# First layer of a hybrid decoder step: one tile shape for neighbouring small products, block-diagonal inverses, sample state update in 32-row tiles

## The chip, the cores and the metric

The kernel runs on one core of one Trainium2 chip. The metric is the device time of one execution in microseconds (us), as a median of runs. Engines are named as in the profile: PE is TensorE's matmul, PEld its weight load, DVE is VectorE, ACT is ScalarE, POOL is GpSimd, SP the queue of SyncE that starts DMAs.

## The reference, cut to what matters

One inference step over two layers, for a prompt of 256 tokens and a sample of 8 batches with 8 tokens each (320 rows together). Only layer 0's mixer matters here: a gated delta net (4 heads of 128) and RWKV-7 (8 heads of 64) side by side. Both are linear recurrences worked out in chunks of 64 tokens: four chunks for the prompt, and one for the sample, in which the eight batches are eight blocks of 8 rows.

```python
# gated delta net, one chunk; RWKV-7 has the same structure with other decays
lmat = jnp.where(strict, bb[..., :, None] * kkt * decay, 0.0)
rhs = bb[..., None] * (vb - gam[..., None] * jnp.einsum('bhck,bhkv->bhcv', kb, s))
u = lax.linalg.triangular_solve(lmat + eye, rhs, left_side=True, lower=True, unit_diagonal=True)
o = gam[..., None] * jnp.einsum('bhck,bhkv->bhcv', qb, s) + jnp.einsum('bhij,bhjv->bhiv', qkt, u)
s_new = jnp.exp(glast)[..., None] * s + jnp.einsum('bhck,bhcv->bhkv', kb * jnp.exp(glast - gcum)[..., None], u)
```

So each chunk needs the inverse of a unit lower triangular 64x64 matrix, products of that inverse with right-hand sides, and a step of the state from chunk to chunk. The sample's states (8 batches) take one step each.

## The kernel before

All weights stream through SBUF in columns of 128. `dense` multiplies them in two float32r parts (hi, lo) with two-part activations: 24 products of 128x128 weights with 256 or 320 columns for each column block. They write the PSUM tiles `pd` and `pe`.

The mixer of layer 0 (`even_in`) lays the small float32 products of the recurrences between those dense ones. After each three dense products `between[0]` runs `step`, which takes the next piece of one of three lanes: `g_lane` (gated delta net, `gdn_unit`, PSUM tag `pG`, tiles `g_...`), `r_lane` (RWKV, `rwkv_solve` and `rwkv_scan`, PSUM tag `pR`, tiles `r_...`) and `set_lane` (`rwkv_setup`). Four units go through each lane. A piece's turn comes by `pe[0]`, an estimate of PE's time that `mm` adds up. PE runs its instructions in this order. A float32 product stands in the trace as two records.

A product's tile shape is written K*M below: K rows of the contraction (partitions of both operands), M columns of the stationary operand (partitions of the output). PE is used in the shapes 128\*128, 128\*64, 64\*128, 64\*64 and 32\*128. The shape follows from the operands' partitions:

- Two chunks share 128 partitions. Chunk c has the rows of half c % 2 (`chunk_rows`), so a product of one chunk alone contracts over 64 rows: K is 64. In `gdn_unit` these are `g_vk` with the inverse, and all products with `g_uw`, the corrected values and keys.
- `solve` inverts by doubling: blocks of 2, 4, ... 64. At each level l it makes two products for each pair of chunks and head, against `n1` and against `t`. For the prompt `u` and `x` hold two chunks in columns of their own between zeros, so K is 128 and M 64. The sample's chunk has tiles of its own (`invs`, `xs`) on 64 partitions, so its products at levels 1 and 2 are 64\*64.
- In `rwkv_scan` a state `z` has one head in each half of the partitions, so its products (`r_zs` with `r_step`, `r_ar` with `r_zs`) are 64\*64, one for each half.
- The sample's state update of the delta net multiplies `kd` (64 rows) with `um`, the corrected values masked to four batches, 64\*128 with 512 columns, twice a unit.

Each unit's results go to `og` and `orw`. When all lanes are done, the output projection starts (`out_proj`, dense again), and with it the fetch of the memory attention's keys and values (`mkv`), which the SP queue issues in program order.

Of the kernel before, what the change touches and what calls it, by code (L numbers as in the profile page):

```python
# [26 lines left out]
def _constants():  # L27
    """Masks and selections that depend on shapes alone: name -> [128, n]."""
# [27 lines left out]
    c["bm8"] = (j[:, None] // 8 == np.arange(8)[None, :]) * 1.0  # L56
    c["sel8"] = (p[:, None] % 32 == np.arange(8)[None, :]) * 1.0
# [12 lines left out]
    even = ("blk64", "triP", "triS", "blkS", "maskP", "maskS", "negP", "negS", "id64", "lev", "lev0T", "bm8", "sel8", "scan")  # L70
# [36 lines left out]
def _lay(inp):  # L107
    """Rearranges the inputs for the device: no arithmetic."""
# [61 lines left out]
def _unlay(r):  # L170
    """Device outputs -> the reference's shapes."""
# [27 lines left out]
def trunk(ctx: ExitStack, tc: tile.TileContext, A, O, phases=None):  # L199
# [86 lines left out]
    def load_log_exp():  # L286
        """The table of Ln and Exp, behind all that was laid out before."""
# [6 lines left out]
    def sigmoid(out):  # L294
        """From out = exp(-x), by functions that share a table."""
# [21 lines left out]
    # ---------------------------------------------------------------- the stream of weights  # L317
# [40 lines left out]
    def weights(kt):  # L358
        """The two parts of the plan's next columns."""
# [6 lines left out]
    def dense(a, kt=KT):  # L366
        """The next 128 columns w of the plan: psum [128, n] = w^T a over kt K-tiles."""
# [5 lines left out]
        if first:  # L373
            # the tensor engine's clock rises with use: zeros keep it at work until the operands are there
# [18 lines left out]
    def split(dst, src, scale=1.0):  # L393
        """dst (hi, lo) = the two parts of src * scale."""
# [37 lines left out]
    class Prep:  # L432
        """Splits x * gain tile by tile for the next products; 1/rms comes later, on their results."""
# [13 lines left out]
    def dense_norm(prep, n, use, kt=KT):  # L447
        """n dense tiles of prep.a; 1/rms is worked out behind the first two of them."""
# [11 lines left out]
    def out_proj(o, nxt):  # L460
        """x += w^T o; the next block's operand is prepared tile by tile."""
# [13 lines left out]
    def weave(main, filler, every=1):  # L475
        """main with a step of the filler after each few of its own, then the filler's rest."""
# [14 lines left out]
    # ---------------------------------------------------------------- feed-forward  # L491
# [88 lines left out]
    # ---------------------------------------------------------------- memory tokens and attention  # L580
# [5 lines left out]
    def mem_kv(layers):  # L586
        """k (feature-major) and v (token-major) of the prompt's memory, into their outputs."""
# [57 lines left out]
    class Mem:  # L645
        """A memory block; its tiles are opened, and the caches' keys fetched, ahead of its turn."""
# [29 lines left out]
    def mem(m, prep, nxt):  # L676
# [17 lines left out]
        def softmax_rows(ps, p):  # L694
            """p = softmax(ps / 16) over the last axis; ps, p [128, nh, 256]."""
# [12 lines left out]
        def s_score(g):  # L708
            # rows (head, batch of four, query): a zero-padded query block for each batch
# [137 lines left out]
    def shaped(a, shape):  # L847
        """a [p, n] seen as [p, *shape]."""
# [3 lines left out]
    def tiles_of(pool, prefix):  # L852
        """t(name, *shape): a tile of a pool in which names share a slot of pad columns by a tag."""
# [13 lines left out]
    def solve(n1, u, x, us, xs, t, bank):  # L867
        """Blocks of 64: the transpose u of (1 - N)^-1 from n1 = N^T + 1 [128, 3, nh, 64], N strictly lower.
        Two chunks share a block of 128 partitions: u and x [128, 2, nh, 2, 64] hold them in columns of their
        own, between zeros, so that one product serves both. The sample's chunk [64, nh, 64] stands alone.  # L870
        At level l the inverses x of blocks of 2^l are joined by pairs; u = x^T changes in the second
        columns of each pair alone, and x, of blocks up to 32, is u with each block of 32 transposed."""
# [3 lines left out]
        def half(a, l, i):  # L876
            """Of the columns of a [..., 64], those with bit l = i."""
# [4 lines left out]
        def pack(a, l):  # L882
            """Their places side by side."""
# [4 lines left out]
        def wide(m, r, n):  # L888
            """A mask or the like [128, ...] for n blocks of rows r."""
# [3 lines left out]
        def views():  # L893
            """Places of 32 columns: the heads' chunks, each head in rows of its own; the sample's."""
            ps = bank()
            return (ps[:, :128].rearrange("p (b o n) -> p b o n", b=2, o=2),
                    ps[:64, 128:128 + 32 * nh].rearrange("p (h n) -> p h n", h=nh))

        low, all_ = H2[0], slice(0, 128)
# [10 lines left out]
        for l in range(1, 6):  # L910
            tt = t()
# [4 lines left out]
            pt, pts = views()  # L916
            for b in two:
                for h in range(nh):
                    mm(pack(pt[H2[h], b].rearrange("p o n -> p (o n)"), l), n1[:, b, h], half(x[:, b, h], l, 0))
            for h in range(nh):  # L920
                for o in two:
                    V.tensor_mul(half(tt[H2[o], :2, h], l, 0), pack(pt[H2[h], :, o], l), wide(lev, H2[h], 2))
            if l < 3:
# [1088 lines left out]
```

## Time and profile before

| | before |
|---|---|
| median of 3 runs | 1482.69 us (1482.44 to 1484.91) |
| profiled execution: span from first to last instruction | 1481.2 us |
| PE busy / PEld busy | 1420.0 us (96%) / 1240.4 us (84%) |
| DVE / ACT / POOL busy | 915.3 / 671.0 / 280.8 us |
| mean granted TensorE clock | 0.954 |

The profiled execution is the only one with a trace, and its span is its time; the runs' median is 1.5 us above it. A busy PE is not PE at its peak: matmuls are pipelined, and a record's duration overlaps the next record's. How fast PE goes through products is read from the starts of neighbouring records. The granted clock is 1.0 at 2.4 GHz and 0.5 at 1.2 GHz; a value between them is a mean over a stretch that has both.

### The profile page before, as it was taken

Reading aid. Unit: us, or ns where it says so; the run is one execution under the profiler, and the core shown is the slowest. Engines: PE = TensorE matmul, PEld = TensorE weight load, DVE = VectorE, ACT = ScalarE, POOL = GpSimd, SP = SyncE. Lnnn points to the kernel's source line nnn. Section 1 sums busy time; section 2 is a strip of 40 time slices with the busy share of each in tenths; the row PEclk is TensorE's granted clock in tenths of the full one; section 3 lists DMA queues with packets and bytes.
Section 4 is the critical chain, followed back from the end, with each engine's and each line's share of the span. In section 5 each row is a group of like instructions: output and inputs, shape, how many; then the busy total and the mean of one; then the engine's idle time right before and its main releaser. Section 6 shows DMA issues by size and latency. Waiting matters only on the chain. (4 is left out here: it accounts for less than half of the span.)

```text
span 1481.2 us, 29014 instructions
## 1 busy us (share of the span) xinstructions
PE 1420.0 (96%) x11071; PEld 1240.4 (84%) x11071; DVE 915.3 (62%) x1916; ACT 671.0 (45%) x1497; POOL 280.8 (19%) x542
## 2 busy tenths in 40 slices
PE   8999999999999899999999999999789999999997
PEld 7798787786896796999999997766359879999997
DVE  6986864764854553566656646684765545666564
ACT  6745434254443442544434535563354335444343
POOL 5532531432411200111100110003011001110001
PEclk9999988889988899999999999999789999999999
DMA  5333232133522856444576747998959644444443
GB/s 215 121 106 119 85 96 80 46 106 94 194 86 64 310 202 264 133 152 152 179 228 204 236 142 269 337 344 298 405 186 383 212 196 145 155 142 157 146 146 100
DMA packets 81485, 268.04 MB, mean 181 GB/s; under 512 B 9346, under 2 KB 21890, under 8 KB 76866
## 3 DMA queue, kind: packets, MB, share of 16 engines
q1 hardware_dynamic: 64450, 247.21, 48.9%
q10 hardware_dynamic: 16896, 18.98, 3.9%
q8 instruction: 87, 1.43, 0.4%
q14 instruction: 52, 0.43, 0.1%
HBM read 254.26 MB, written 11.90 MB: 180 GB/s over the span
## 5 line engine op out<-in xcount | busy, mean ns | idle before, releaser
L284 ACT ACTIVATE whi<-raw 128x512 fp32r<-128x512 f32 (+1 forms) x541 | 308.0, 616 | 382.7 <-PE pd L270 160.8
L344 DVE TENSOR_TENSOR wlo<-raw,whi 128x512 fp32r<-128x512 f32 (+1 forms) x541 | 383.0, 745 | 81.0 <-ACT whi L284 78.4
L270 PE MATMUL pd<-ahi,whi 128*128 128x320 f32 (+2 forms) x1336 | 420.2, 316 | 9.1 <-ACT ahi L284 5.0
L270 PE MATMUL pd<-ahi,wlo 128*128 128x320 f32 (+1 forms) x1328 | 416.4, 314 | 3.7 <-DVE wlo L344 3.6
L270 PE MATMUL pd<-alo,whi 128*128 128x320 f32 (+2 forms) x1336 | 416.8, 315 | 2.1 <-DVE alo L301 2.1
L270 PEld LDWEIGHTS pd<-ahi,whi 128*128 128x128 f32 (+1 forms) x1336 | 257.7, 193 | 22.2 <-ACT ahi L284 6.8
L270 PEld LDWEIGHTS pd<-ahi,wlo 128*128 128x128 f32 x1328 | 256.9, 193 | 14.0 <-issue 6.1
L270 PEld LDWEIGHTS pd<-alo,whi 128*128 128x128 f32 (+1 forms) x1336 | 256.3, 193 | 14.2 <-issue 7.1
L270 PE MATMUL pe<-alo,whi 128*128 128x320 f32 x416 | 129.7, 312 | 0.0
L270 PE MATMUL pe<-ahi,wlo 128*128 128x320 f32 x416 | 129.1, 310 | 0.5 <-DVE wlo L344 0.5
L270 PE MATMUL pe<-ahi,whi 128*128 128x320 f32 x416 | 128.7, 310 | 0.0
L519 POOL TENSOR_TENSOR fw<-fw 128x320 f32<-128x320 f32 x44 | 39.0, 886 | 332.9 <-DVE fw L518 303.6
L420 POOL TENSOR_TENSOR acc<-acc,w 128x320 f32<-128x320 f32 (+1 forms) x48 | 47.2, 982 | 240.2 <-ACT w L284 237.9
L270 PEld LDWEIGHTS pe<-ahi,wlo 128*128 128x128 f32 x416 | 78.1, 188 | 1.5 <-DVE wlo L344 1.4
L270 PEld LDWEIGHTS pe<-alo,whi 128*128 128x128 f32 x416 | 78.1, 188 | 0.5
L270 PEld LDWEIGHTS pe<-ahi,whi 128*128 128x128 f32 x416 | 78.0, 188 | 0.3
L270 PE MATMUL pe<-fhi,whi 128*128 128x320 f32 x176 | 54.3, 309 | 0.0
L270 PE MATMUL pd<-fhi,whi 128*128 128x320 f32 x176 | 54.3, 309 | 0.0
L270 PE MATMUL pe<-fhi,wlo 128*128 128x320 f32 x176 | 54.3, 309 | 0.0
L270 PE MATMUL pe<-flo,whi 128*128 128x320 f32 x176 | 54.3, 309 | 0.0
L270 PE MATMUL pd<-fhi,wlo 128*128 128x320 f32 x176 | 54.3, 309 | 0.0
L270 PE MATMUL pd<-flo,whi 128*128 128x320 f32 x176 | 54.3, 309 | 0.0
(460 smaller groups left out, 2283.4 us busy)
## 6 DMA issues: line engine op xcount, KB each, us to landing
pg<-in_kv SPq DMA_DIRECT2D x107, 512.0 KB, 6.6
raw<-in_w_fi SPq DMA_DIRECT2D x88, 512.0 KB, 3.6
mkv<-in_mkv SPq DMA_DIRECT2D x32, 1024.0 KB, 9.3
raw<-in_w_fo SPq DMA_DIRECT2D x32, 512.0 KB, 3.6
raw<-in_w_sb SPq DMA_DIRECT2D x24, 512.0 KB, 3.7
raw<-in_w_gp SPq DMA_DIRECT2D x16, 512.0 KB, 3.5
raw<-in_w_mk SPq DMA_DIRECT2D x16, 512.0 KB, 3.6
raw<-in_w_mv SPq DMA_DIRECT2D x16, 512.0 KB, 3.6
```

The costliest lines, as they stand in the source:

```text
L270: nc.tensor.matmul(out, lhsT=lhsT, rhs=rhs, start=start, stop=stop, skip_group_check=True)
L284: S.activation(out, in_, f, **kw)
L344: V.tensor_sub(lo[:, ks], raw[:, ks], hi[:, ks])
L420: P.tensor_add(self.acc, self.acc, self.sq)
L519: P.tensor_mul(u, u, st["g"])
```

## The change

Products that stand beside each other get the same tile shape, by operands that are padded with zeros to all 128 partitions:

- `solve` takes the sample's chunk as a third block of the same tiles `u` and `x`, with zeros in the upper 64 rows of `n1`, `u` and `t`. Its products are 128\*64, and its masks, copies and first transposes are done with those of the prompt.
- In `gdn_unit` the inverses of both chunks of a pair, side by side, are one stationary of 128\*128 (`both`). `uw` is one tile for all units with a place for each half and zeros beside it, so all products of the scan are 128\*128. `rows` and `sel` are padded from 8 to 128 rows.
- In `rwkv_scan` the corrections use the pair's inverse as 128\*128, and `z` becomes two column blocks, each head's state with zeros in the other head's rows: products of 128\*64. Its final write is two DMAs instead of one.
- The sample's state update masks `uv` once, by the batch's place in its half (`bm4`), and multiplies 32 rows with 32 rows: two products of 32\*128.

Comments and docstrings are dropped too, which the diff below leaves out.

```diff
-    def solve(n1, u, x, us, xs, t, bank):
+    def solve(n1, u, x, t, bank):
...
-        for o in two:
-            P.memset(u[H2[o], :, :, 1 - o], 0.0)
+        P.memset(u[H2[0], :, :, 1], 0.0)
+        P.memset(u[H2[1], :, :, 0], 0.0)
+        P.memset(u[H2[1], 2, :, 1], 0.0)
         for h in range(nh):
             for o in two:
-                r = H2[o]
-                V.tensor_mul(u[r, :, h, o], n1[r, :2, h], wide(cc("lev0T"), r, 2))
-            V.transpose(x[:, :, h], u[:, :, h])
-        V.tensor_mul(us, n1[low, 2], wide(cc("lev0T"), low, nh))
-        V.transpose(xs, us)
+                nb = 3 - o
+                V.tensor_mul(u[H2[o], :nb, h, o], n1[H2[o], :nb, h], wide(cc("lev0T"), H2[o], nb))
+        V.transpose(x, u)
...
+            if nb == 3:
+                P.memset(tt[H2[1], 2], 0.0)
...
-            for b in two:
+            pt = bank()
+            for b in range(nb):
                 for h in range(nh):
-                    mm(pack(pt[H2[h], b].rearrange("p o n -> p (o n)"), l), n1[:, b, h], half(x[:, b, h], l, 0))
+                    y = x[:, b, h] if b < 2 else x[:, b, h, 0]
+                    mm(pack(place(pt, h, b), l), n1[:, b, h], half(y, l, 0))
...
-                for h in range(nh):
-                    mm(pack(pts[:, h], l), n1[low, 2, h], half(xs[:, h], l, 0))
-                V.tensor_mul(half(tt[low, 2], l, 0), pack(pts, l), wide(lev, low, nh))
...
+            if l < 2:
+                V.transpose(x, u)
...
+            uw = st_even["uw"] = ep.tile([128, 2, 2, 2, 128], F32, name="g_uw")
+            for o in range(2):
+                P.memset(uw[H2[1 - o], :, o], 0.0)
...
-        for c in range(4):
-            r, b, cs = chunk_rows(c)
-            mm(pu[r, b].rearrange("p a n -> p (a n)"), inv[r, b, 0, c % 2], vk[r, b].rearrange("p a n -> p (a n)"))
-        act(uw, pu)
+        for b in range(2):
+            mm(pu[:, b].rearrange("p a n -> p (a n)"), both(b), vk[:, b].rearrange("p a n -> p (a n)"))
+        act(uw[H2[0], :, 0], pu[H2[0]])
+        V.tensor_copy(uw[H2[1], :, 1], pu[H2[1]])
...
-            mm(pz, kd[r, b], uw[r, b, 0], stop=c == 0)
+            mm(pz, kd[:, b], uw[:, b, o, 0], stop=c == 0)
...
-            um = t("um", 4, 128)[:64]
-            P.tensor_mul(um, bc(uv[:64, None, :], [64, 4, 128]), bc(cc("bm8")[:64, b4, None], [64, 4, 128]))
-            yield 1.2
+            b4, rows4 = slice(4 * q, 4 * q + 4), slice(32 * q, 32 * q + 32)
             pz = bank_g()
-            mm(pz, kd[:64, 2], um.rearrange("p b n -> p (b n)"))
+            mm(pz, kd[rows4, 2], um[rows4].rearrange("p b n -> p (b n)"))
...
+        pu = bank_r()[:, :512].rearrange("p (b h n) -> p b h n", b=2, h=2)
+        for b in range(2):
+            for h in range(2):
+                mm(pu[:, b, h], inv[:, b, h].rearrange("p o n -> p (o n)"), rhs[:, b, h].rearrange("p a n -> p (a n)"))
         for odd in range(2):
             rr = h2[odd]
-            pu = bank_r()[:, :512].rearrange("p (b h n) -> p b h n", b=2, h=2)
-            for b in range(2):
-                for h in range(2):
-                    mm(pu[rr, b, h], inv[rr, b, h, odd], rhs[rr, b, h].rearrange("p a n -> p (a n)"))
...
-                        mm(pz[h2[h]], step[h2[h], c - 1], z[h2[h]], start=False)
+                        mm(pz[h2[h]], step[:, c - 1], z[:, h], start=False)
...
-            z = t("zs", 64, bufs=2)
-            ts(z, pz, fac[:, c:c + 1], None, ALU.mult)
+            z = t("zs", 2, 64, bufs=2)
+            stt(z, bc(pz[:, None, :], [128, 2, 64]), fac[:, c:c + 1], cc("blk64").rearrange("p (h n) -> p h n", h=2),
+                ALU.mult, ALU.mult)
```

The order of instructions shows where PE's shape changes. First PE in the solve of unit 0, levels 1 and 2 of the inversion, of the kernel before. The sizes are those of the output; `r_xs`, `r_invs` and the 64x32 rows are the sample's, 64\*64, the `pd` rows are 128\*128, the others 128\*64.

```order
L270 MATMUL pd<-alo,whi 128x256
L270 MATMUL pR<-r_invs,r_t 64x32 x2
L270 MATMUL pR<-r_xinv,r_n_890 64x64
L270 MATMUL pG<-g_ux,g_t 64x32
L270 MATMUL pR<-r_xinv,r_n_890 64x64 x3
L270 MATMUL pG<-g_ux,g_n_1152 64x64 x2
L270 MATMUL pd<-ahi,whi 128x256
```

The same place of the changed kernel, where the sample's products follow those of the prompt, all 128\*64:

```order
L271 MATMUL pd<-alo,whi 128x256
L271 MATMUL pR<-r_inv,r_t 64x64
L271 MATMUL pd<-ahi,whi 128x256
L271 MATMUL pR<-r_inv,r_t 64x64 x3
L271 MATMUL pR<-r_inv,r_t 64x32 x2
L271 MATMUL pG<-g_ux,g_t 64x64 x2
L271 MATMUL pG<-g_ux,g_t 64x32
L271 MATMUL pd<-ahi,wlo 128x256
```

Five changes of shape became four, two of them around a single dense product that stands inside the group. The second place is the end of the mixer, unit 3, on PE of the kernel before: the corrections of RWKV (`r_rhs`, 64\*64) and of the delta net (`g_vk`, 64\*64).

```order
L270 MATMUL pR<-r_rhs,r_inv 64x128 x8
L270 MATMUL pR<-cst,r_sa 64x128
L270 MATMUL pR<-r_sav,r_g 64x64 x2
L270 MATMUL pG<-g_vk,g_ux 64x256 x4
L275 MATMUL pG<-cst,g_sa 64x128
```

And of the changed kernel:

```order
L271 MATMUL pR<-r_rhs,r_inv 128x128
L271 MATMUL pR<-cst,r_sa 64x128
L271 MATMUL pR<-r_sav,r_g 64x64 x2
L271 MATMUL pR<-r_rhs,r_inv 128x128 x3
L271 MATMUL pG<-g_vk,g_ux 128x256 x2
```

Twelve products became six of twice the output rows, and one of the four `r_rhs` products moved ahead of the sample's. The third place is the last six small products before the output projection, before:

```order
L270 MATMUL pR<-orw,cste 128x320
L270 MATMUL pR<-r_sm,r_bkt 64x512
L270 MATMUL pG<-g_um,g_kd 128x512
L270 MATMUL pR<-w,cste 128x320
L270 MATMUL pR<-r_s_151,r_lora 128x320
L270 MATMUL pG<-g_um,g_kd 128x512
L270 MATMUL pG<-w,cst 128x320
```

and now, where the two updates of the sample's states stand together:

```order
L271 MATMUL pR<-orw,cste 128x320
L271 MATMUL pR<-r_sm,r_bkt 64x512
L271 MATMUL pG<-g_um,g_kd 128x512 x2
L271 MATMUL pR<-w,cste 128x320
L271 MATMUL pR<-r_s_154,r_lora 128x320
L271 MATMUL pG<-w,cst 128x320
```

Counted over PE's whole instruction order of the mixer, up to its last small product: 473 changes of tile shape between neighbours before and 316 now, 988 small products before and 964 now. The `g_um` pair is adjacent in two units of the four. DVE has 44 instructions fewer in the whole kernel, ACT has 20 activations fewer and 4 DMAs more, POOL has 48 more, nearly all of them fills with zeros.

## Rows read from the trace of the kernel before

**Rows 1.** The page, the span in 40 equal slices of 37 us: PE's busy tenths, and the granted clock in tenths.

```profile
PE   8999999999999899999999999999789999999997
PEclk9999988889988899999999999999789999999999
```

**Rows 2.** Busy time by stretch. The columns are: from and to (us), length, busy us of PE, PEld, DVE, ACT and POOL with their instructions, granted clock, share of the DMA engines, GB/s.

```profile
8.00:490.00 482.00, 467.80 (x3390) 381.66 (x3388) 328.44 (x839) 228.69 (x604) 166.84 (x345) 0.90 0.33 106
...
60.00:82.00 22.00, 21.13 (x144) 17.70 (x143) 20.86 (x52) 12.20 (x27) 12.89 (x25) 1.00 0.41 135
82.00:92.00 10.00, 10.00 (x74) 9.70 (x75) 5.97 (x18) 1.22 (x4) 4.79 (x11) 0.68 0.19 61
181.00:209.00 28.00, 28.00 (x210) 25.46 (x209) 20.07 (x60) 11.36 (x28) 11.12 (x23) 0.76 0.26 85
243.00:273.00 30.00, 28.68 (x157) 18.36 (x156) 13.75 (x44) 9.45 (x27) 9.99 (x24) 0.55 0.08 22
403.00:420.00 17.00, 17.00 (x98) 14.92 (x98) 8.22 (x23) 2.29 (x5) 3.18 (x6) 0.60 0.14 46
468.00:490.00 22.00, 18.69 (x42) 8.01 (x42) 7.02 (x15) 4.91 (x9) 6.24 (x7) 0.50 0.11 42
490.00:495.00 5.00, 4.48 (x15) 4.08 (x16) 1.90 (x2) 0.20 (x1) 0.96 (x1) 0.50 0.88 287
```

**Rows 3.** Waits of PE from 8 to 490 us, the longest: who waited for whom, total us, times, longest.

```profile
PE pd L270 <- DVE r_e L1311: 2.6, 2, 1.8
```

**Rows 4.** PE in order of time at 2.4 GHz: start, us until the end, product, K*M, moving operand, records. Two groups of small products of one shape, the second between dense ones.

```profile
116.98 0.45 PE L270 MATMUL pR<-r_inv,r_t 128*64 128x64 f32 x8
117.26 0.40 PE L270 MATMUL pG<-g_ux,g_t 128*64 128x64 f32 x4
...
129.68 0.31 PE L270 MATMUL pd<-alo,whi 128*128 128x320 f32 x1
129.83 0.31 PE L270 MATMUL pd<-ahi,whi 128*128 128x320 f32 x1
130.06 0.45 PE L270 MATMUL pR<-r_xinv,r_n 128*64 128x64 f32 x8
130.35 0.40 PE L270 MATMUL pG<-g_ux,g_n 128*64 128x64 f32 x4
130.67 0.42 PE L270 MATMUL pd<-ahi,wlo 128*128 128x320 f32 x1
130.93 0.31 PE L270 MATMUL pd<-alo,whi 128*128 128x320 f32 x1
131.07 0.31 PE L270 MATMUL pd<-ahi,whi 128*128 128x320 f32 x1
```

**Rows 5.** The same view at three more places: the scan of unit 0, the last unit's corrections, and the sample's state update.

```profile
150.82 0.38 PE L270 MATMUL pG<-g_sc,g_step 128*128 128x128 f32 x2
151.14 0.43 PE L270 MATMUL pG<-g_g,g_uw 64*128 64x64 f32 x2
151.50 0.43 PE L270 MATMUL pG<-g_kq,g_sc 128*128 128x64 f32 x2
151.86 0.48 PE L270 MATMUL pG<-g_uw,g_kd 64*128 64x128 f32 x2
152.28 0.34 PE L270 MATMUL pR<-r_sav,xT 128*64 128x64 f32 x4
152.54 0.33 PE L270 MATMUL pR<-r_zs,r_step 64*64 64x64 f32 x4
152.81 0.34 PE L270 MATMUL pR<-xT,r_sav 128*64 128x64 f32 x4
...
456.32 1.36 PE L270 MATMUL pR<-r_rhs,r_inv 64*64 64x128 f32 x16
457.61 0.43 PE L270 MATMUL pR<-cst,r_sa 128*64 128x128 f32 x2
...
164.09 1.12 PE L270 MATMUL pG<-g_um,g_kd 64*128 64x512 f32 x2
165.14 0.41 PE L270 MATMUL pd<-alo,whi 128*128 128x320 f32 x1
```

**Rows 6.** The first products of the kernel, which multiply zeros (`zero`): PE in order of time, then two stretches with the columns of the second group (the number of PE records stands in brackets).

```profile
3.41 5.31 PE L270 MATMUL pd<-zero 128*128 128x320 f32 x12 [3.41 <-POOL r_e L1307]
...
3.50:7.00 3.50, 3.50 (x7) 2.32 (x8) 1.20 (x2) 1.64 (x4) 0.08 (x2) 1.00 0.93 339
7.00:8.30 1.30, 1.30 (x6) 0.88 (x6) 0.51 (x4) 1.30 (x4) 0.97 (x2) 1.00 1.04 415
```

**Rows 7.** PE in order of time where the clock has just fallen: a long run of narrow products, and two dense ones of 256 columns.

```profile
183.65 1.13 PE L270 MATMUL pR<-r_ar,r_z 64*64 64x16 f32 x16
...
189.42 0.41 PE L270 MATMUL pd<-ahi,whi 128*128 128x256 f32 x1
189.63 0.41 PE L270 MATMUL pd<-ahi,wlo 128*128 128x256 f32 x1
```

**Rows 8.** Groups of instructions from 8 to 490 us: a transpose at the start of `solve`, and a fill with zeros; behind the count the busy us and the mean ns of one, then the idle time ahead of them.

```profile
L906 DVE STREAM_TRANSPOSE r_xinv<-r_inv 128x256 f32<-128x256 f32 x8 | 3.0, 409 | 0.0
...
L901 POOL MEMSET r_inv<- 64x256 f32 x8 | 2.4, 305 | 14.7 <-PE pR L270 14.5
```

**Rows 9.** The end of the mixer: PE's first product of the output projection, and the first fetch for the memory attention on the SP queue.

```profile
490.25 0.64 PE L270 MATMUL pd<-ahi,whi 128*128 128x320 f32 x1 [3.56 <-ACT ahi L284]
...
491.93 0.33 SPq L662 DMA_DIRECT2D mkv<-in_mkv  x1
```

More of the change, by code (lines that the diff above doesn't have):

```diff
@@ L69, in _constants @@
     c["causal"] = np.where(p[None, :] < p[:, None], 0.0, NEG)
[L70 removed]
+    even = ("blk64", "triP", "triS", "blkS", "maskP", "maskS", "negP", "negS", "id64", "lev", "lev0T", "bm8", "bm4", "sel8", "scan")
     groups = []
@@ L920, in solve @@
+            pt = bank()
+            for b in range(nb):
+                for h in range(nh):
+                    y = x[:, b, h] if b < 2 else x[:, b, h, 0]
+                    mm(pack(place(pt, h, b), l), n1[:, b, h], half(y, l, 0))
             for h in range(nh):
                 for o in two:
-                    V.tensor_mul(half(tt[H2[o], :2, h], l, 0), pack(pt[H2[h], :, o], l), wide(lev, H2[h], 2))
-            if l < 3:
-                P.tensor_copy(half(tt[low, 2], l, 1), wide(one, low, nh))
-                for h in range(nh):
-                    mm(pack(pts[:, h], l), n1[low, 2, h], half(xs[:, h], l, 0))
-                V.tensor_mul(half(tt[low, 2], l, 0), pack(pts, l), wide(lev, low, nh))
@@ L928, in solve @@
-            yield HOP
-            pu, pus = views()
-            for b in two:
-                for h in range(nh):
-                    mm(pack(pu[H2[h], b].rearrange("p o n -> p (o n)"), l), tt[:, b, h], half(u[:, b, h], l, 1))
+                    n = nb if o == 0 else 2
+                    src = pt[H2[h], :64 * n].rearrange("p (b n) -> p b n", n=64)[:, :, 32 * o:32 * o + 32]
+                    V.tensor_mul(half(tt[H2[o], :n, h], l, 0), pack(src, l), wide(lev, H2[h], n))
+            yield HOP
@@ L933, in solve @@
+            pu = bank()
+            for b in range(nb):
+                for h in range(nh):
+                    y = u[:, b, h] if b < 2 else u[:, b, h, 0]
+                    mm(pack(place(pu, h, b), l), tt[:, b, h], half(y, l, 1))
             for h in range(nh):
                 for o in two:
-                    act(half(u[H2[o], :, h, o], l, 1), pack(pu[H2[h], :, o], l))
-                if l < 5:
-                    V.transpose(x[:, :, h], u[:, :, h])
-            if l < 3:
-                for h in range(nh):
-                    mm(pack(pus[:, h], l), tt[low, 2, h], half(us[:, h], l, 1))
-                act(half(us, l, 1), pack(pus, l))
-                if l < 2:
-                    V.transpose(xs, us)
+                    n = nb if o == 0 else 2
+                    src = pu[H2[h], :64 * n].rearrange("p (b n) -> p b n", n=64)[:, :, 32 * o:32 * o + 32]
+                    act(half(u[H2[o], :n, h, o], l, 1), pack(src, l))
+                if l < 5 and l > 1:
+                    V.transpose(x[:, :2, h], u[:, :2, h])
@@ L1096, in gdn_stats @@
             tr(pr[:8, 128 * b:128 * b + 128], rt[:, b])
-        rows = [ep.tile([8, NT], F32R, name=f"g_rows{i}") for i in range(2)]
-        split(rows, pr[:8, :NT])
+        rows = [ep.tile([128, NT], F32R, name=f"g_rows{i}") for i in range(2)]
+        for x in rows:
+            P.memset(x.bitcast(F32), 0.0)
+        split([x[:8] for x in rows], pr[:8, :NT])
         st_even.update(beta=beta, gcum=gcum, dec=dec, nbg=nbg, rows=rows)
@@ L1220, in gdn_unit, with both @@
         yield 0.8
-        ux = t("ux", 640, tag="kb")
-        inv, xinv = (shaped(ux[:, 256 * i:256 * i + 256], (2, 1, 2, 64)) for i in range(2))
-        invs, xs = (shaped(ux[:64, 512 + 64 * i:576 + 64 * i], (1, 64)) for i in range(2))
-        yield from solve(n1, inv, xinv, invs, xs, lambda: t("t", 3, 1, 64, bufs=2), bank_g)
+        ux = t("ux", 768, tag="kb")
+        inv, xinv = (shaped(ux[:, 384 * i:384 * i + 384], (3, 1, 2, 64)) for i in range(2))
+        yield from solve(n1, inv, xinv, lambda: t("t", 3, 1, 64, bufs=2), bank_g)
         oT = og[:, u]
-        uw = t("uw", 2, 2, 128)
-        pu = [bank_g().rearrange("p (b a n) -> p b a n", b=2, a=2) for _ in range(1)][0]
-        for c in range(4):
-            r, b, cs = chunk_rows(c)
-            mm(pu[r, b].rearrange("p a n -> p (a n)"), inv[r, b, 0, c % 2], vk[r, b].rearrange("p a n -> p (a n)"))
-        act(uw, pu)
+        def both(b):
+            return inv[:, b, 0].rearrange("p o n -> p (o n)")
+        uw = st_even["uw"]
+        pu = bank_g().rearrange("p (b a n) -> p b a n", b=2, a=2)
+        for b in range(2):
+            mm(pu[:, b].rearrange("p a n -> p (a n)"), both(b), vk[:, b].rearrange("p a n -> p (a n)"))
+        act(uw[H2[0], :, 0], pu[H2[0]])
+        V.tensor_copy(uw[H2[1], :, 1], pu[H2[1]])
         yield 0.3
@@ L1253, in gdn_unit @@
         pu = bank_g()
-        mm(pu[:64, :128], invs[:, 0], r1[:64])
+        mm(pu[:, :128], both(2), r1)
         uv = t("uv", 128)
-        act(uv[:64], pu[:64, :128])
+        act(uv, pu[:, :128])
         yield HOP
@@ L1556, in rwkv_scan @@
                 for h in range(2):
-                    mm(py[h2[h]], z[h2[h]], ar[h2[h], c, 1], start=False)
+                    mm(py[h2[h]], z[:, h], ar[:, c, 1], start=False)
             act(yT[:, cs], py)
-            z = t("zs", 64, bufs=2)
-            ts(z, pz, fac[:, c:c + 1], None, ALU.mult)
+            z = t("zs", 2, 64, bufs=2)
+            stt(z, bc(pz[:, None, :], [128, 2, 64]), fac[:, c:c + 1], cc("blk64").rearrange("p (h n) -> p h n", h=2),
+                ALU.mult, ALU.mult)
             yield HOP
-        S.dma_start(O["rwkv_p"][:, 64 * u:64 * u + 64], z)
+        for h in range(2):
+            S.dma_start(O["rwkv_p"][h2[h], 64 * u:64 * u + 64], z[h2[h], h])
         pz = bank_r()
```

66 lines of the change are left out of this document (38 added, 28 removed).

## Prediction

> **What bounds the kernel now.** I read the page's 40 slices first. PE is at 0.9 nearly everywhere, and the granted clock is below 0.9 in slices 6 to 9 and 12 to 14, and later in two more [rows 1]. The first thirteen slices are layer 0's mixer, the only part that the change touches. The stretch from 8 to 490 us says more: PE is busy for 467.80 of 482.00 us, so it idles for 14.2; DVE has 328.44, ACT 228.69, POOL 166.84; the clock is 0.90 [rows 2]. A clock of 0.90 means that (1 - 0.90) x 2 = 0.2 of the stretch, about 96 us, ran at 1.2 GHz. So PE is the bound, and its time holds two things beside plain work: the changes of shape between small products, and the slow clock. In two places another engine is near: from 60 to 82 us DVE is busy for 20.86 of 22.00 us [rows 2], and the longest waits of PE are for DVE's `r_e`, 2.6 us in two [rows 3]; and at the end of the mixer PE idles 3.56 us before the output projection [rows 9].
>
> What the mixer saves, the kernel saves: `mkv`'s fetch stands on SP behind the mixer, at 491.93 [rows 9], and the dense work after it follows in PE's order. So I look for one number, by how much 490 moves.
>
> **The price of a change of shape.** The rows of starts give it. Dense products follow each other at 0.15 us (129.68 to 129.83). From 129.83 there is an excursion to small products and back: dense, eight records of `r_xinv`, four of `g_ux`, dense, dense, up to 130.93: 1.10 us [rows 4]. Without the two changes it would take 2 x 0.147 for the two dense ones, 0.28 for eight records (116.98 to 117.26, where a group of the same shape follows), and the four. For those I have bounds: half of eight, 0.14, or by the pace of a 512-column record, 1.05 / 2 = 0.53 us (164.09 to 165.14 [rows 5]), so 0.066 for 64 columns and 0.26 for four. What is left is 0.27 to 0.39, or 0.135 to 0.195 a change. The scan gives the same by another way: at 150.82, 151.14, 151.50 and 151.86 runs of two records, each of another shape than the one before, take 0.32, 0.36, 0.36 and 0.42; at the 512-column pace (0.13 for two of 64 columns, 0.27 for two of 128) 0.05, 0.23, 0.23 and 0.15 are left, 0.165 on average [rows 5]. I take 0.15, in the middle of both.
>
> **Work that goes.** The order has 157 changes of shape fewer: 157 x 0.15 = -23.6 us. `r_rhs`, sixteen records of 64\*64 from 456.32 to 457.61, takes 1.29, of which I leave out 0.10 for the change behind it; as four products of 128\*128 it is eight records of 128 columns, by the 512-column pace 8 x 0.13 = 1.05; four units: 4 x (1.05 - 1.19) = -0.6. The two 32\*128 products of the sample's update are neighbours in two of the four units and use different rows of the array; I take it that they overlap, and then each such pair saves one product of 1.05: -2.1. If they don't, nothing. The sample's products in `solve` had a group of their own and now ride with the others; that lies in the 157, and their count hardly moves. The padded `g_rows`, `g_uw` and `z` products keep their columns, and I price them as unchanged: in [rows 5] the 64\*128 run at 151.14 and the 128\*128 run at 151.50, 64 columns each, take 0.36 both. With 24 products fewer in all I add -2 for what the list leaves out (bounds 0 and -4). Sum of the work: -23.6 - 0.6 - 2.1 - 2 = **-28 us**. Bounds: with the lowest single remainder, 0.05, for all 157, -8 and nothing else; with 0.195, -30.6 - 0.6 - 2.1 - 4 = -37.
>
> **Clock.** Where are the 96 us at 1.2 GHz? By stretch: 82 to 92 has 0.68, 181 to 209 0.76, 403 to 420 0.60, which makes 6.4 + 13.4 + 13.6 = 33 us; there the clock falls after runs of narrow products that the change leaves as they are (`r_ar,r_z`, 64\*64 with 16 columns, sixteen records in 1.13 us at 183.65 [rows 7]). 243 to 273 has 0.55 and 468 to 495 has 0.50, which makes 27 + 27 = 54 us [rows 2]; there it falls after solves, corrections and scans of 64\*64 and 64\*128, which now get 128 rows. That zeros count as work for the clock is seen at the start: products of `zero` ran at seven records in 3.5 us and then six in 1.3 us, so they are what ran while the clock came up [rows 6]. Dense products of 256 columns follow at 0.21 us in the slow clock (189.42 to 189.63 [rows 7]), against 0.147 x 256/320 = 0.118 at full: 44% of such time is lost. All of the 54 us back would be -24; none, 0; and since stretches can also move to other places, a loss of 0.44 x 20 = +9 can't be excluded. I take 38 of the 54 us: 38 x 0.44 = **-17 us**.
>
> **Waits that come.** `solve` now transposes the whole tile in one instruction before the first product, where the first product needed one third. One piece of 256 columns takes 0.41 us, so the whole 1.23, and the first product waits 0.8 longer [rows 8]. It happens up to twice in each of eight solves: 16 x 0.8 = 13 us if PE had nothing else; but dense products stand between the pieces, and PE waits for `solve`'s tiles hardly at all now, since `r_e` heads the list with 2.6 us [rows 3]. I take 3 of the 13. From 60 to 82 us DVE sets the pace: PE's share of the saving there, 22/482 of 45 = 2, comes back as waiting. At the end, where 3.56 us are idle already [rows 9], less PE work meets the same chain of DVE and ACT: 3. Sum **+8 us**, bounds 0 and 18 (33 with the fills that follow). POOL's 48 more instructions at 0.3 us [rows 8] are 14.6 us, beside 315 us in which POOL idles; they cost nothing as long as each fill precedes its first reader by a few us, and up to the 14.6 if every one was waited for. ACT's four more DMA issues and DVE's 44 fewer instructions change nothing on the path.
>
> **Sum.** -28 - 17 + 8 = -37: the span goes from 1481.2 to 1444.2. The median of the runs lies 1.5 us above the profiled time; so 1445.7, **1446 us**.
>
> **Rivals.**
> - *The clock stays as it is.* For it: the clock in the mixer falls in places that have nothing to do with scans too, and less time in small products also means that the runs of narrow ones come closer together. Against it: 54 of 96 us follow products that change. Then -28 + 8 = -20: 1462.7.
> - *Clock all back, no waits.* -28 - 24 = -52: 1430.7, and less with the dearer change of shape.
> - *Waits eat half.* 18 us of waiting, with the work at its low bound and the forecast clock: -8 - 17 + 18 = -7, or, without the clock, -28 + 18 = -10; so 1473 to 1476. For it: the transposes and DVE at 60 to 82 us; against it: 14.2 us of idle time in 482.
> - *Nothing comes of it.* The runs of two records in the scan are 0.36 apart because each waits for the result of the one before, not for a shape. Then the 157 are worth little, and the clock's return is taken by the waits: 1480 to 1485. Against it: the excursion at 129.83 has no such dependence, as its products are those of two lanes, and shows the same price.
> - *Slower: padding costs double.* Padded products use 128 rows where 64 did, so two that ran side by side on different rows now run in a row. They take now: in the scan 0.36 + 0.42 + 2 x 0.26 = 1.3 us a chunk, 16 chunks, 20.8; `r_rhs` 1.29 x 4 = 5.2; together 26 us. With work and waits alone (-20) the kernel is slower from 1.8 times their present time on; at twice, 1481.2 - 20 + 26 = 1487.2, 1488.7 as a median. Against it: the scan's products depend on each other, so the halves already run in turn, and the 64- and 128-row runs of equal columns at 151.14 and 151.50 are equally far apart [rows 5].
>
> The Trainium skill, "TensorEngine Tiling (Array Packing)", § Performance Considerations, advises the reverse of this change: for a contraction of up to 64 rows, two tiles of 64 rows, which its overview puts at up to twice the speed. By that rule the padded products would take up to double, which is the last rival. The same page, § Tiling Modes, says that a change of the tiling mode drains the engine, without a price; the remainders in [rows 4, 5] agree with it. The page's two rules pull apart, and by the rows the second is the larger here.
>
> **How the numbers follow.** A measurement of this kernel can tell about 0.2%, 3 us, from no change. The forecast, between 1431 and 1458, gets 0.55; the clock all back, below 1431, 0.10; the clock stays, 1458 to 1468, 0.17; waits eat half, 1468 to 1479, 0.06; nothing comes of it, 0.05; slower, 0.07. Faster: 0.55 + 0.10 + 0.17 + 0.06 = 0.88. The range from 1424 to 1472 leaves out 0.03 below, and above about half of the waits (0.03), 0.05 and 0.07: 0.18.
>
> **What would show it.** The output projection's first product and `mkv`'s fetch at about 453 instead of 490. In the scan, runs of two records of one shape 0.13 to 0.27 apart, where they stood at 0.32 to 0.42. The clock of the mixer at 0.93 or more, with 243 to 273 at 0.9 and the stretches after `r_ar,r_z` still low. PE's idle time in the mixer at about 22 us, with waits for `r_inv` and `g_ux` in the list. `g_um` as a pair within about 1.1 us. The prediction is wrong if the padded products take longer than the changes of shape that they save, or if the list of waits is headed by the transposed tiles with over 20 us.

## The result and the profile after

| | before | after |
|---|---|---|
| median of 6 runs each | 1481.41 us | 1438.61 us (1430.73 to 1441.99) |
| ratio | | 0.971 (95% interval 0.966 to 0.976) |
| profiled execution: span | 1481.2 us | 1429.0 us |
| mean granted clock of it | 0.954 | 0.978 |

The kernel is 43 us faster by the medians. A second set of runs of the same two kernels gave 1475.78 to 1438.74, ratio 0.972 (0.969 to 0.976). The forecast was 37 us less. The profiled executions are 52 us apart, more than the medians are: the profile of after is the fastest of its six runs and the one with the highest clock (0.978, the others 0.970 to 0.974).

PE and the granted clock in the 40 slices of the page of after, to be held beside [rows 1]:

```profile
PE   7899998999998999999999999998889999999997
PEclk9999999999999999999999999997889999999999
```

The two dips of the clock in the first third are gone in this execution. Busy time by stretch of after, with the columns of [rows 2]: the whole mixer, DVE's stretch at 60 us, two stretches behind narrow products, one that had the clock at 0.55, and the end of the mixer.

```profile
8.00:436.00 428.00, 404.33 (x3348) 346.79 (x3346) 328.31 (x794) 223.72 (x583) 177.32 (x380) 0.99 0.37 119
60.00:82.00 22.00, 19.69 (x140) 17.35 (x139) 20.86 (x51) 11.84 (x27) 13.91 (x26) 1.00 0.39 130
82.00:92.00 10.00, 10.00 (x100) 9.36 (x100) 6.93 (x17) 2.66 (x6) 5.52 (x12) 1.00 0.22 73
181.00:209.00 28.00, 28.00 (x266) 25.44 (x264) 23.14 (x59) 14.13 (x37) 14.46 (x32) 1.00 0.34 106
243.00:273.00 30.00, 27.95 (x182) 21.70 (x181) 26.79 (x57) 11.28 (x28) 17.52 (x39) 0.94 0.25 81
425.00:440.00 15.00, 9.72 (x45) 6.22 (x44) 8.54 (x14) 4.96 (x8) 6.17 (x7) 0.78 0.38 126
```

The mixer is 54 us shorter, PE's busy time 63 us, and PE idles 428.00 - 404.33 = 23.7 us where it idled 14.2. DVE is as busy as before, to 0.1 us. The first row gives the split, with the prediction's 44% for lost time in the slow clock. Before: 482 x 0.20 x 0.44 = 42.4 us lost, so 467.80 - 42.4 = 425.4 of work at full clock. After: 428 x 0.02 x 0.44 = 3.8, so 400.6. Work -24.8, clock -38.6, waits +9.5: -53.9, and the rest of the kernel +1.7. The clock's two digits leave about 2 us open on either side.

Where the work went is seen in PE's rows of after, in order of time: the scan's runs of two records, the corrections of the last unit, the sample's update, and the start of the output projection; last, the first fetch for `mkv` on SP.

```profile
141.48 0.33 PE L271 MATMUL pG<-g_g,g_uw 128*128 128x64 f32 x2
141.65 0.44 PE L271 MATMUL pG<-g_kd,g_uw 128*128 128x128 f32 x2
141.93 0.33 PE L271 MATMUL pG<-g_g,g_uw 128*128 128x64 f32 x2
...
412.60 0.49 PE L271 MATMUL pR<-r_rhs,r_inv 128*128 128x128 f32 x2
413.02 0.43 PE L271 MATMUL pR<-cst,r_sa 128*64 128x128 f32 x2
413.29 0.40 PE L271 MATMUL pR<-r_sav,r_g 128*64 128x64 f32 x4
413.61 0.94 PE L271 MATMUL pR<-r_rhs,r_inv 128*128 128x128 f32 x6
414.38 1.03 PE L271 MATMUL pG<-g_vk,g_ux 128*128 128x256 f32 x4
...
262.92 1.13 PE L271 MATMUL pG<-g_um,g_kd 32*128 32x512 f32 x4
263.98 0.41 PE L271 MATMUL pd<-alo,whi 128*128 128x320 f32 x1
...
436.34 0.64 PE L271 MATMUL pd<-ahi,whi 128*128 128x320 f32 x1 [5.13 <-ACT ahi L285]
...
439.30 0.33 SPq L663 DMA_DIRECT2D mkv<-in_mkv  x1
```

Runs of two records now stand 0.17 us (64 columns) and 0.28 us (128 columns) apart, where [rows 5] has 0.32 to 0.42. The pair of `g_um` takes 1.06 us, as much as one product took. The fetch of `mkv` came 52.6 us earlier than in [rows 9], and the kernel ended 52.2 earlier.

The waits of PE from 8 to 436 us of after, for [rows 3]:

```profile
PE pR L276 <- DVE r_zs L302: 2.7, 2, 1.9
PE pd L271 <- DVE r_e L1329: 2.6, 2, 1.8
PE pR L271 <- ACT r_w L285: 2.0, 3, 1.2
PE pR L276 <- DVE r_bk L1437: 1.6, 1, 1.6
...
PE pG L271 <- DVE g_ux L946: 1.1, 1, 1.1
...
PE pR L271 <- DVE r_t L933: 0.5, 2, 0.3
...
PE pR L271 <- DVE r_xinv L948: 0.4, 1, 0.4
PE pG L271 <- DVE g_t L933: 0.2, 1, 0.2
```

The transpose of a whole tile at the start of `solve` in after, with the columns of [rows 8]:

```profile
L910 DVE STREAM_TRANSPOSE r_xinv<-r_inv 128x768 f32<-128x768 f32 x4 | 3.8, 960 | 0.0
```

### The profile page after: what moved, and what is told of

The parts are those of the page before. It is cut to its first block, busy times and chain, and to the rows that moved or that the text cites. A ratio compares the mean times of both kernels' runs of the same rounds, so it can differ in the third digit from the quotient of the medians.

```text
span 1429.0 us, 28913 instructions
## 1 busy us (share of the span) xinstructions
PE 1359.8 (95%) x11023; PEld 1208.5 (85%) x11023; DVE 916.2 (64%) x1872; ACT 667.7 (47%) x1477; POOL 294.8 (21%) x590
## 5 line engine op out<-in xcount | busy, mean ns | idle before, releaser
L271 PE MATMUL pd<-ahi,wlo 128*128 128x320 f32 (+1 forms) x1328 | 410.4, 309 | 2.0 <-DVE wlo L345 2.0
L271 PE MATMUL pd<-alo,whi 128*128 128x320 f32 (+2 forms) x1336 | 410.8, 310 | 0.9 <-DVE alo L302 0.8
L271 PEld LDWEIGHTS pd<-ahi,whi 128*128 128x128 f32 (+1 forms) x1336 | 252.7, 189 | 24.0 <-ACT ahi L285 7.3
L271 PEld LDWEIGHTS pd<-alo,whi 128*128 128x128 f32 (+1 forms) x1336 | 251.6, 189 | 11.7 <-issue 6.8
L271 PEld LDWEIGHTS pd<-ahi,wlo 128*128 128x128 f32 x1328 | 252.1, 190 | 10.7 <-DVE wlo L345 3.9
```

The lines of the kernel that those rows point to most:

```text
L271: nc.tensor.matmul(out, lhsT=lhsT, rhs=rhs, start=start, stop=stop, skip_group_check=True)
```

## The experiments

The question is how the 43 us divide into changes of shape, clock and the rest. Theory A is the prediction's: a change of shape costs PE about 0.15 us, and zero rows cost nothing. Theory B: the changes cost nothing themselves, only the clock gains. The third is padding that costs double.

**One part at a time.** The changed kernel is four parts; three were put alone into the kernel before. The solve alone (the sample's chunk as third block; scans and updates as before):

```diff
-                    mm(pack(pts[:, h], l), n1[low, 2, h], half(xs[:, h], l, 0))
+            for b in range(nb):
+                for h in range(nh):
+                    y = x[:, b, h] if b < 2 else x[:, b, h, 0]
+                    mm(pack(place(pt, h, b), l), n1[:, b, h], half(y, l, 0))
```

> The kernel before with the padded solve alone: the sample's chunk is a third block of the pair's tiles; scans, corrections and the sample's state update as before. The order of PE in the mixer has 77 changes of shape fewer (396 for 473) and as many products. Theory A (a change of shape costs PE about 0.15 us, zero rows cost nothing): work down by 77 x 0.15 = 11.6 us, PE's waits up by up to 3 us for the transposes of the whole tile, so about -9 us at an unchanged clock. Theory B (the gain is the clock's alone): PE's time outside the slow clock stays, and the span moves only with the time at 1.2 GHz. For the clock, if it is the scans' and corrections' rows that let it fall, the stretches behind the scans at 246 to 273 and 468 to 495 us stay slow here, and the kernel gains no more than the 9 us; if it is the stalls of PE at the changes of shape, they shorten here too.

The delta net alone:

```diff
-            mm(pz, kd[r, b], uw[r, b, 0], stop=c == 0)
+            mm(pz, kd[:, b], uw[:, b, o, 0], stop=c == 0)
```

> The kernel before with the padded delta net alone: the pair's inverse as one 128*128 stationary, the padded values and keys, the padded rows for the gates; solve, RWKV and the sample's state update as before. 55 changes of shape fewer (418). Theory A: 55 x 0.15 = 8.3 us less work at an unchanged clock. Theory B: nothing but the clock. The rival of padding that costs double would lose here: the padded products' present 13 us would grow to up to 26 and the kernel would be 5 us slower. For the clock: if wide rows matter, the slow stretches behind the scans shorten here and in the RWKV part, not with the solve.

The RWKV scan alone:

```diff
-                        mm(pz[h2[h]], step[h2[h], c - 1], z[h2[h]], start=False)
+                        mm(pz[h2[h]], step[:, c - 1], z[:, h], start=False)
```

> The kernel before with the padded RWKV scan alone: corrections by the pair's inverse as 128*128, the state in two columns of 64 between zeros; the rest as before. 58 changes of shape fewer (415), 16 products fewer. Theory A: 58 x 0.15 + 0.6 = 9.3 us less work at an unchanged clock. Theory B: nothing but the clock. Padding that costs double: 13 us of padded products would grow to up to 26, and the kernel would be 4 us slower. For the clock as with the delta net's part.

The whole change beside them on the same chip:

> The changed kernel once more, beside its parts on the same chip. Theory A: 157 changes of shape fewer make 23.6 us, less than the sum of the parts' 190, since parts share changes; with 4 to 5 us of other work and about 10 us more of waits -19 us at an unchanged clock, and the rest of the 43 us that the median fell is the clock. Theory B: at an unchanged clock nothing is gained.

Measured against 11 runs of the kernel before on the same chip (1475.78 us): the solve 0.986 (0.983 to 0.989), the delta net 0.988 (0.984 to 0.992), RWKV 0.988 (0.983 to 0.992), all together 0.972. To take the clock out, I use the runs themselves. In the 28 runs of the kernel before whose clock is on record, span and mean clock go together (correlation -0.91), 1.24 us of span for 0.001 of clock; a single run lies some 2 us off that line. With that each part is brought to the clock of before:

| kernel | median span, us | median clock | clock's share | the rest | changes of shape less x 0.15 |
|---|---|---|---|---|---|
| before | 1474.0 | 0.957 | | | |
| solve alone | 1455.8 | 0.963 | -7.5 | -10.7 | 77: -11.6 |
| delta net alone | 1458.4 | 0.963 | -7.5 | -8.2 | 55: -8.3 |
| RWKV alone | 1455.6 | 0.965 | -10.0 | -8.5 | 58: -8.7 |
| all | 1437.0 | 0.971 | -17.4 | -19.6 | 157: -23.6 |

The rest of each single part is near its count of changes times 0.15. That they agree within 1 us is luck: with each run brought to the clock of before ahead of taking the medians, the rests are -13.2, -8.7, -9.0 and -21.2, so a rest is known to some 3 us, and a change of the single parts comes to 0.14 to 0.17 us. The whole kernel's rest, for which -19 was expected, holds 7 to 9 us of waits as well. Theory B, a rest of zero, has fallen, and so has padding that costs double, which would have put the delta net and RWKV above the kernel before. The mixers of the profiled executions say the same (start and end of the mixer, columns of [rows 2]; in this order the solve, the delta net, RWKV, all):

```profile
8.00:463.00 455.00, 439.43 (x3394) 365.89 (x3392) 330.44 (x791) 226.74 (x588) 180.53 (x388) 0.93 0.35 112
...
8.00:461.00 453.00, 435.94 (x3378) 367.90 (x3376) 335.64 (x844) 228.78 (x604) 167.69 (x345) 0.95 0.35 113
...
8.00:460.00 452.00, 433.12 (x3360) 361.76 (x3358) 329.91 (x839) 228.18 (x600) 171.26 (x345) 0.96 0.34 113
...
8.00:444.00 436.00, 414.89 (x3348) 357.14 (x3346) 328.44 (x794) 223.91 (x583) 177.04 (x380) 0.96 0.35 117
```

By the working above, 439.43 - 455 x 0.14 x 0.44 = 411.4, and likewise 416.0, 417.2 and 399.5, against 425.4 of before: work down by 14.0, 9.4, 8.2 and 25.9 us, each within some 3 us. The changed kernel had 24.8 in its own profile at a clock of 0.99, and 25.9 here at 0.96: within that, the work is the same from one execution to another, the clock is not. In this second profile the stretch behind the first `r_ar,r_z` is slow, which was at 1.00 in the first, and the clock has fallen at 59 us too, where PE waits for DVE twice (columns of [rows 2], then PE in order of time):

```profile
59.00:62.00 3.00, 2.70 (x10) 2.71 (x11) 3.00 (x6) 2.55 (x6) 3.00 (x3) 0.50 0.48 156
82.00:92.00 10.00, 10.00 (x76) 9.70 (x76) 5.92 (x14) 1.28 (x4) 4.86 (x11) 0.70 0.19 61
...
57.96 0.38 PE L271 MATMUL pd<-alo,whi 128*128 128x256 f32 x1 [0.87 <-DVE alo L302]
59.30 0.63 PE L271 MATMUL pd<-ahi,wlo 128*128 128x320 f32 x1 [0.95 <-DVE wlo L345]
```

What the expectations said of the clock stays open. By the clocks above, 64, 45 and 36 us of the three mixers ran at 1.2 GHz, and with the solve alone the long slow stretch, 246 to 273 us in before, stayed slow:

```profile
233.00:264.00 31.00, 30.08 (x154) 19.59 (x155) 14.34 (x44) 9.31 (x26) 11.13 (x29) 0.51 0.07 21
```

That is what was expected if rows of 64 let the clock fall. But this profile is the run with the lowest clock of its five (0.957), and by the medians the clock came back as much with the solve (0.963) as with the other two (0.963, 0.965), as was expected of the changes of shape. The parts do not say which of them brings the clock back.

**The price by itself.** Series of zero products were put ahead of the first dense one of the kernel before. A first kernel had short series:

```diff
+            sep(); series(24, A1)          # A1: 128*128, 64 columns
+            sep(); series(12, A1, R0)      # R0: 64*128
...
+            sep(); series(8, (q32[0], all4, 512, full))   # 32*128, 512 columns
```

> The kernel before with series of zero products ahead of its first dense one, each series behind ten separators of 96 columns: 24 of one shape, 12 pairs of two shapes in turn (128*128 with 64*128, 128*128 with 128*64, 128*64 with 64*64), products on different rows or columns of the array in turn, and products of 512 columns. The time of the kernel grows by these series and says nothing; read are the starts. Theory A: in a series of two shapes in turn each product takes 0.15 us longer than in a series of one shape. Theory B: the same time as in a series of one shape. For the rival of padding that costs double: products of 64 rows on different rows of the array in turn take half the time of those on the same rows (0.05 for 0.11 us), and two products of 32*128 with 512 columns on different rows take the time of one, about 1.05 us; if they don't overlap, both are the same as on the same rows.

In this kernel the clock itself fell in the first series of two shapes in turn and again in the last, and the second ran in the slow clock throughout. The second kernel was made for that: longer series, each behind sixty 128\*128 products of 256 columns.

```diff
+            sep = lambda: series(60, (all4, all4, 256, full))
+            sep(); series(40, W5)          # 128*128, 512 columns
+            sep(); series(40, V5)          # 64*128, the same rows
+            sep(); series(40, V5, V6)      # 64*128, both halves of the rows in turn
+            sep(); series(50, A1, R0)      # 64 columns: 128*128 and 64*128 in turn
+            sep(); series(50, A1, C0)      # 128*128 and 128*64 in turn
+            sep(); series(160, A1)
+            sep(); series(300, D0)         # 64*64
+            sep(); series(300, C0)         # 128*64
+            sep(); series(300, D0, D1)     # 64*64, both corners in turn
+            sep(); series(50, C0, D0)      # 128*64 and 64*64 in turn
```

> The kernel before with longer series of zero products ahead of its first dense one, each behind sixty 128*128 products of 256 columns that bring the clock back: 512 columns on 128 rows, on the same 64 rows, and on two halves of the rows in turn; 64-column products of two shapes in turn; 64-column products of one shape. Read are the starts and the granted clock of each series. If stalls at the changes of shape make the clock fall, it falls in the three series of two shapes in turn and holds in all of one shape, the 64-row ones too. If unused rows make it fall, it falls in the series of 512 columns on the same 64 rows, holds on 128 rows and on both halves in turn, and in the series of 128*128 and 128*64 in turn as well. Price of a change at the full clock, by the parts' runs: 0.15 us.

Its stretches, in the order of the list (the columns of [rows 2]; PEld's number in brackets is that of the records started; the series of two shapes in turn are cut where the clock fell):

```profile
32.11:66.17 34.06, 34.06 (x81) 14.98 (x80) 0.00 (x0) 0.00 (x0) 0.00 (x0) 1.00 0.00 0
92.82:126.98 34.16, 34.16 (x80) 14.86 (x80) 0.00 (x0) 0.00 (x0) 0.00 (x0) 1.00 0.00 0
153.83:188.00 34.17, 34.17 (x161) 15.30 (x160) 0.00 (x0) 0.00 (x0) 0.00 (x0) 1.00 0.00 0
214.75:219.30 4.55, 4.55 (x27) 3.73 (x25) 0.00 (x0) 0.00 (x0) 0.00 (x0) 1.00 0.00 0
219.30:272.70 53.40, 53.40 (x175) 43.16 (x175) 0.00 (x0) 0.00 (x0) 0.00 (x0) 0.50 0.00 1
...
301.36:308.00 6.64, 6.64 (x45) 5.22 (x43) 0.00 (x0) 0.00 (x0) 0.00 (x0) 1.00 0.00 0
308.00:348.00 40.00, 40.00 (x158) 30.85 (x157) 0.00 (x0) 0.00 (x0) 0.00 (x0) 0.50 0.00 0
376.46:412.00 35.54, 35.54 (x320) 35.54 (x319) 0.00 (x0) 0.00 (x0) 0.00 (x0) 1.00 0.01 1
438.42:473.40 34.98, 34.98 (x600) 34.98 (x600) 0.00 (x0) 0.00 (x0) 0.00 (x0) 1.00 0.01 2
499.89:534.90 35.01, 35.01 (x601) 35.01 (x600) 0.00 (x0) 0.00 (x0) 0.00 (x0) 1.00 0.01 2
561.36:596.30 34.94, 34.94 (x1199) 34.94 (x1200) 0.00 (x0) 0.00 (x0) 0.00 (x0) 1.00 0.02 4
622.83:628.90 6.07, 6.07 (x49) 4.52 (x48) 0.00 (x0) 0.00 (x0) 0.00 (x0) 1.00 0.01 3
628.90:659.40 30.50, 30.50 (x153) 21.59 (x153) 0.00 (x0) 0.00 (x0) 0.00 (x0) 0.50 0.00 1
```

A product is two records. Alone, 128\*128 takes 2 x 35.54/320 = 0.222 us, 64\*64 and 128\*64 take 2 x 34.98/600 = 0.117. In turn, at the full clock: 128\*128 with 64\*128 2 x 4.55/25 = 0.364, which is 0.14 more than the 0.222 of 128\*128. The 64\*128 product of 64 columns was timed alone in the first kernel only, in the slow clock: 2 x 10.40/48 = 0.433, about twice the 0.222, so I take it for as long as 128\*128.

```profile
59.10:69.50 10.40, 10.40 (x49) 10.31 (x48) 0.00 (x0) 0.00 (x0) 0.00 (x0) 0.50 0.01 2
```

The other two pairs at the full clock: 128\*128 with 128\*64 2 x 6.64/43 = 0.309, 0.14 more than the mean of the two, 0.170; 128\*64 with 64\*64 2 x 6.07/48 = 0.253, 0.14 more than 0.117. So a change costs 0.14 us at the full clock in all three pairs, and each product in turn pays one. In the slow clock the same series take 2 x 53.40/175 = 0.610, 0.510 and 0.399 us a product, so 37 to 40% of slow time is lost in them, where the split above has 44% from dense products and the slope of the 28 runs gives 42%. With 37%, some 6 us of that split would be work and not clock.

For the clock: in all seven series of one shape it stayed at full, 34 to 36 us each, the ones on 64 rows and on a quarter of the array too. In all three series of two shapes in turn it fell to 1.2 GHz within the series and stayed there to its end. So in these series the changes of shape let it fall, and not the rows and columns that the shapes leave unused. That PE stands still at a change is read from the starts; the profile has it busy throughout.

The same list shows what padding gives up: eighty products of 64\*128 on two halves in turn take 34.17 us, as long as forty on the same rows. They overlap fully, and so do 64\*64 products on two corners (1200 records in the time of 600). Of the padded products, `r_rhs`'s hardly used that: sixteen records of 64\*64 took 1.29 us with the first half of them on one half of the rows [rows 5], and now eight records of 128\*128 take 0.42 + 0.77, a change or two included. The `r_zs` products did run on two corners, four records in 0.27 us with a change [rows 5]. Padded to 128\*64, the two heads stand on the two halves of the columns, and four records take 0.17 us in after, less than the 4 x 0.058 = 0.23 of products on one half: they still overlap.

```profile
145.59 0.34 PE L271 MATMUL pR<-r_zs,r_step 128*64 128x64 f32 x4
145.76 0.29 PE L271 MATMUL pR<-xT,r_sav 128*64 128x64 f32 x4
```

**The sample's update.** Alone in the kernel before, once and then in twelve runs, and taken out of the changed kernel:

```diff
-            mm(pz, kd[:64, 2], um.rearrange("p b n -> p (b n)"))
+            mm(pz, kd[rows4, 2], um[rows4].rearrange("p b n -> p (b n)"))
```

> The kernel before with the sample's state update of the delta net in 32-row tiles alone, adjacent in three of the four units. If tiles on different rows overlap, an adjacent pair takes about 1.1 us for the 2.1 that its two products take one by one, about 3 us less in all; if they don't, nothing changes but the shape, and the kernel stays as it is. POOL has four masks fewer. Nothing of it moves the slow stretches.

> The sample's state update in 32-row tiles alone, once more with rounds: its one look was 19 us faster than the run of before beside it, with 58 us at 1.2 GHz in the mixer where the profile of before has 97 and nearly the same work. If that was the chance of the clock, the medians lie within 5 us of each other; if the part moves the clock, it stays 10 us or more faster. Work alone: 4 changes of shape less and three adjacent pairs that overlap, -0.6 and -3 us.

> The changed kernel with the sample's state update of the delta net as it was (64*128, masked to four batches at a time). 339 changes of shape where the changed kernel has 316: 23 x 0.15 = 3.5 us more, two pairs that no longer overlap 2.1 us more, some 2 us of slow clock more: about 7 us slower than the changed kernel (0.977 of the kernel before instead of 0.972). If 32-row tiles gain nothing, the same as the changed kernel.

The first execution took 1464.45 beside 1483.75, which looked like 19 us. Twelve runs give 0.994 (0.991 to 0.997), 1472.53 for 1480.26: 8 us, between the sizes that stood for chance (within 5) and for a cause (10 or more). The clock's median (0.9575 for 0.955) is 3 of them and the rest 5. Forecast were 3.6 with three adjacent pairs; the traces have two, in units 1 and 3, which makes 2.7. In the first execution one of them stands at the full clock and takes 1.06 us:

```profile
288.59 1.13 PE L271 MATMUL pG<-g_um,g_kd 32*128 32x512 f32 x4
289.65 0.43 PE L271 MATMUL pR<-cst,r_ar 128*64 128x128 f32 x2
```

Most of the 19 us was the chance of one execution's clock. The changed kernel without this part has 0.977 (0.973 to 0.981), 1443.51 us: 5 us above the changed kernel's 1438.74, where 7 were expected. The two ran on different chips and their intervals overlap (0.969 to 0.976 with the part), so this difference by itself is not clear of noise.

## Why the prediction was right

- **The changes of shape** were the largest term, 157 x 0.15 = 23.6. Measured: 0.14 each at the full clock by the series, and 0.14 to 0.17 by the parts alone. With 0.14 the sum without its allowance is 22.0 + 0.6 + 2.1 = 24.7, and the work as a whole fell by 24.8 and 25.9 in two profiles, known to some 3 us; so the allowance of 2 us for what the list left out was probably too much. The price was read from remainders of 0.05 to 0.23, which scatter because the pace of 512 columns is too fast for 64. With the runs' own pace in after (0.17 and 0.28) the four are 0.04, 0.19, 0.19 and 0.14, with a mean of 0.14.
- **The clock** was taken as -17 and is -17.4 by the medians of the second set of runs (of the first set only one run of before has its clock on record). The reason given was wrong in part. The prediction ascribed the falls to products of 64 rows and said that the stretches behind `r_ar,r_z` would stay slow. In the profile of after the first two of them came back (82 to 92 and 181 to 209 us at 1.00). In the second profile the first of them is slow again, and the clock also falls where PE waits. The series show that changes of shape can let the clock fall, and rows of 64 alone do not. That the changes are the cause in the mixer is likely but not shown. That the size fits is luck in part: more stretches can come back than were counted, and in most executions not all do. Between the two profiles alone it was 38.6. The start of the kernel doesn't show that zeros count, either: [rows 6] has a granted clock of 1.00 in both stretches, whatever changed the pace there. The series do, as products of zeros kept it at 1.00 for 34 us.
- **The waits** were +8 and are +9.5 (+6.9 in the second profile). Their places were others. The transposes of the whole tile took 0.96 to 0.97 us for 768 columns, not 1.23, and PE waited for `solve`'s tiles 2.2 us in all (`g_ux`, `r_t`, `r_xinv`, `g_t`), with 3 in the sum. PE idles instead where lanes reach each other: `r_zs`, `r_w`, `r_bk`, and the chain at the end, 5.13 us where 3.56 stood in [rows 9]. From 60 to 82 us PE idles 2.3 us instead of 0.9, with DVE at 20.86 us in both; the sum had 2 more.
- **The slower rival** has a real mechanism, since products on different rows do overlap fully. But this kernel's order put products of one half behind each other, or behind results, or kept the overlap on the columns, so nothing was lost. The page of the Trainium skill that advises 64-row tiles, "TensorEngine Tiling (Array Packing)", § Performance Considerations, is right where such tiles run side by side: twice the speed in the second kernel of series. The same page of the Trainium skill, § Tiling Modes, says that a change of tiling mode drains the engine. The series agree that a change costs PE time, 0.14 us; whether it is a drain they can't show.
- **The parts don't add up.** Alone they drop 77 + 55 + 58 + 4 = 194 changes, together 157: two padded groups side by side share a border with the dense products that one alone also removes.

## What to carry to other kernels

Where small products stand between dense ones, count the changes of tile shape in PE's order and multiply by a measured price; here 0.14 us each, as much as a dense product of 320 columns. Zero rows cost nothing here, where the columns are the same and no second half would have run beside them. A single profile is a poor measure of what a change does to the clock: bring runs to the same clock first, by the slope of the kernel's own runs.

## What the runs showed of the hardware

In the series, changes of shape between products are enough to let the clock fall, though PE looks busy all the time; the prediction had not expected that, and the share of busy time doesn't show it. Two series contradict a simple rule, in the first kernel of series (columns as before): sixteen records of 64\*128 with 512 columns, begun in the slow clock, and sixteen of 32\*128, begun at full.

```profile
118.16:132.10 13.94, 13.94 (x17) 5.16 (x16) 0.00 (x0) 0.00 (x0) 0.00 (x0) 0.50 0.00 0
...
136.56:147.30 10.74, 10.74 (x17) 3.87 (x16) 0.00 (x0) 0.00 (x0) 0.00 (x0) 0.65 0.00 0
```

The 64\*128 products did not bring the clock back, though in the second kernel they kept it for 34 us, and the 32\*128 products, of one shape, lost it. So the changes of shape are not the only thing that lets it fall; what let it fall in the 32\*128 series and what it needs to rise again stays open, and so does why the same program gets a clock of 0.948 in one execution and 0.963 in another.
